# Row factors of the feed-forward parts: one product with a 128x128 block of ones, the Newton steps on all partitions

## The chip, the cores and the metric

One core of one Trainium2 chip runs the kernel. The metric is the device time of one execution in microseconds (us). Three executions of the kernel before took 2188.64, 2190.5 and 2190.98 us; the median is 2190.5 us.

## What is computed

A decoder of two layers over 512 tokens of width 1024, in float32. Each layer is a feed-forward part, a token mixer and a second feed-forward part. Every part begins with an RMS norm: each token (a row of x) is divided by the root of the mean of its squares.

```python
def rms_norm(x, w):
    y = xf * lax.rsqrt(jnp.mean(xf * xf, axis=-1, keepdims=True) + NORM_EPS)
    return y * w

def swiglu_ffn(h, wg, wu, wd):
    return (jax.nn.silu(h @ wg) * (h @ wu)) @ wd

for l in range(DEPTH):
    x = x + 0.5 * swiglu_ffn(rms_norm(x, ffn1_norm[l]), ...)
    x = x + mixed(rms_norm(x, mix_norm[l])) @ w_out[l]
    x = x + 0.5 * swiglu_ffn(rms_norm(x, ffn2_norm[l]), ...)
return rms_norm(x, final_norm)
```

The feed-forward width is 2816. The reciprocal root of a row is a number for each token, and is called its row factor here.

## The kernel before

x stands transposed: eight tiles `x0` to `x7` of 128 features (partitions) by 512 tokens. Matrix products are made in three passes on rounded halves: `xh`, `xl` of x times the norm's weight, and `hi`, `lo` of the weights, so that each 128x128 block of weights costs three products (`mm3`, L217). The row factor is left out of `xh` and `xl`. It is applied to the products: `gated` multiplies `pg` (the gate product in PSUM) by `rstd` on VectorE (`g<-pg,rstd`), takes the silu on ScalarE, multiplies by `rstd` again on GpSimd, and multiplies `pu` (the up product) by the result on VectorE (`u<-pu,g`). `rstd` is therefore a tile of 128x512 with each token's factor in all 128 partitions.

How `rstd` comes about: `square` sums the squares of the eight x tiles into `acc` (128x512). `stats_tok` makes four products with `acc` as the stationary operand and a 128x64 block of 1/1024 (`ones_d`) as the moving one, which gives the mean squares with tokens on partitions (`ps_ms`). It then takes the reciprocal root on VectorE, by a shift and a subtraction on the bits and three Newton steps, on tiles of 128x4 (`ms`, `rs_t`, `rstd_tok`; 12 instructions). `stats_rows` brings the factors back to the layout of the products: four products of `rstd_tok`, broadcast over 128 columns, with the identity (`ps_rb`, L423), and a copy by ScalarE (`rstd<-ps_rb`). Both functions serve the four feed-forward parts and the two mixers; a mixer needs `rstd_tok` for its own products too.

A feed-forward part (`ffn`) goes through the 22 blocks of 128 hidden features in three groups of 8, 8 and 6. For each block `f` TensorE makes `pg` and `pu`, 24 products each, and after a group the eight `pd` (down product), which VectorE adds to x. Some queues matter:

- The products of a group lie in PSUM in a ring of three buffers (`pa`); only in the first group, while `rstd` is not yet there, a few go to a second ring (`pb`). In the first group `hold` is 1 (2 in the very first part): the block 0 products `pg` and `pu` and the block 1 `pg` take the three buffers of `pa`, the block 1 `pu` goes to `pb`, and the block 2 `pg` takes the buffer of the block 0 `pg` again. It can begin only when `g<-pg,rstd` of block 0 has read that buffer.
- Weights come by DMA into `raw`, two blocks at a time; ScalarE rounds a block to `hi` and VectorE (seldom GpSimd) makes `lo<-raw,hi` (`split`). Both have rings of four buffers, so the `hi` of one block waits until TensorE is done with the block four earlier in the order pg0, pu0, pg1, pu1, pg2, ...
- Each engine works through its instructions in one order, fixed when the program is built by the framework's scheduler from priorities and a timeline of its own. `stats_tok` runs under a high priority.

Of the kernel before, what the change touches and what calls it, by code (L numbers as in the profile page):

```python
# [10 lines left out]
F32 = mybir.dt.float32  # L11
# [4 lines left out]
ALU = mybir.AluOpType  # L16
# [3 lines left out]
P = 128  # L20
D = 1024
KD = D // P
T = 512
# [4 lines left out]
EPS = 1e-6  # L28
# [137 lines left out]
class Kern:  # L166
# [9 lines left out]
    def pool(self, name, bufs, **k):  # L176
        return self.tc.tile_pool(name=name, bufs=bufs, reuse_waits="tile", **k)
# [218 lines left out]
    def rsqrt(self, out, v, shape):  # L396

        nc = self.nc
        t = self.tiny.tile(shape, F32, tag="rs_t", name="rs_t")
        nc.vector.tensor_scalar(t.bitcast(I32), v.bitcast(I32), 1, None, ALU.logical_shift_right)  # L400
        nc.vector.tensor_scalar(out.bitcast(I32), t.bitcast(I32), -1.0, 1597463007.0, ALU.mult, ALU.add)
        f = lambda a: a.rearrange("p a b -> p (a b)")
        for _ in range(3):
            nc.vector.tensor_tensor(t, out, out, ALU.mult)
            nc.vector.scalar_tensor_tensor(f(t), f(t), -0.5, f(v), ALU.mult, ALU.mult)
            nc.vector.scalar_tensor_tensor(f(out), f(t), 1.5, f(out), ALU.add, ALU.mult)

    def stats_tok(self):
        nc = self.nc
        with self.tc.high_priority(offset=4000):  # L410
            ps = self.pb.tile([P, NT, 64], F32, tag="b", name="ps_ms")
            for t in range(NT):
                nc.tensor.matmul(ps[:, t, :], self.acc[:, t * P:(t + 1) * P], self.ones_d, start=True, stop=True)
            v = self.tiny.tile([P, NT, 1], F32, tag="ms", name="ms")
            nc.vector.tensor_scalar(v, ps[:, :, 0:1], EPS, None, ALU.add)
            self.rstd_tok = self.tiny.tile([P, NT, 1], F32, tag="rstd_tok", name="rstd_tok")
            self.rsqrt(self.rstd_tok, v, [P, NT, 1])

    def stats_rows(self):
        nc = self.nc  # L420
# [26 lines left out]
    def ffn(self, wg, wu, wd, layer, norm, meanwhile=None, begun=None):  # L447
        nc = self.nc
        xs = list(self.xs)
        for gi, (f0, nf) in enumerate(GROUPS):  # L450
            act, queue = [], deque()
            gu, uu = self.gate_up(wg, wu, gi) if gi or not begun else begun

            hold = 0 if gi else 2 if begun else 1
            for f in range(nf):
                where = lambda i: (self.pb, "b") if 3 <= 2 * f + i <= 2 * hold + 1 else (self.pa, "a")
                pool, tag = where(0)
                pg = pool.tile([P, T], F32, tag=tag, name="pg")
                self.mm3(pg, next(gu), xs, KD)
                if hold and f == hold:  # L460
                    self.stats_rows()
                    while queue:
                        queue.popleft()()
                pool, tag = where(1)
                pu = pool.tile([P, T], F32, tag=tag, name="pu")
                self.mm3(pu, next(uu), xs, KD)
                if hold and f == 0:
                    self.stats_tok()
                queue.append(lambda pg=pg, pu=pu: act.append(self.gated(pg, pu)))
                if f >= hold:  # L470
                    queue.popleft()()
            if gi == 0 and meanwhile:
                with self.tc.issue_after(self.last_load.ins):
                    meanwhile()
            last = gi == len(GROUPS) - 1
            if last and layer == DEPTH:
                return self.end(lambda: self.dense_units(wd[f0 * P:(f0 + nf) * P, :], nf, at=NARROW), act, nf)
            for d, dw in enumerate(self.dense_units(wd[f0 * P:(f0 + nf) * P, :], nf)):
                pd = self.pb.tile([P, T], F32, tag="b", name="pd")
                self.mm3(pd, dw, act, nf)  # L480
                nc.vector.scalar_tensor_tensor(self.x[d], pd, 0.5, self.x[d], ALU.mult, ALU.add)
                if last:
                    self.prepare(d, self.sv[layer][norm])
# [939 lines left out]
    def run(self):  # L1423
        nc, tc, io = self.nc, self.tc, self.io
        with ExitStack() as ctx:
            pool = lambda name, bufs, **k: ctx.enter_context(self.pool(name=name, bufs=bufs, **k))
            dram = ctx.enter_context(tc.tile_pool(name="dram", bufs=1, space=bass.MemoryType.DRAM))
            self.xd = [[dram.tile([P, T], F32, name=f"xd{l}_{d}") for d in range(KD)] for l in range(DEPTH)]
            self.const = pool("const", 1)
            self.pad = pool("pad", 1)  # L1430
            self.pad.tile([P, PAD], F32, name="pad")
            self.xsp = pool("xsp", 1)
            self.wraw = pool("wraw", 2)
            self.whi = pool("whi", W_BUFS)
            self.wlo = pool("wlo", W_BUFS)
            self.tmp = pool("tmp", 1)
            self.m = pool("m", M_BUFS)
            self.mb = pool("mb", 1)
            self.tiny = pool("tiny", 2)
            self.conv = pool("conv", 2)  # L1440
            self.pa = pool("pa", 3, space=PSUM)
            self.pb = pool("pb", 5, space=PSUM)
            self.xs = [None] * KD
            self.new_x()
            self.cst = self.const.tile([P, CST.shape[1]], F32, name="cst")
            self.msk = self.const.tile([P, MSK.shape[1]], U8, name="msk")
            self.ones_d = self.const.tile([P, 64], F32, name="ones_d")
            nc.gpsimd.memset(self.ones_d, 1.0 / D)
            nc.sync.dma_start(self.c("ident"), io["cst"][:, 0:P])
            self.first_vectors()  # L1450
            xt = {}
            begun = self.gate_up(io["ffn1_w_gate"][0], io["ffn1_w_up"][0], 0, 2, (1 if FIRST else 0, 0))
            first = []
            for g in range(2):
                for t in range(NT):
                    xt[t, g] = self.t2("xt")
                    nc.sync.dma_start(xt[t, g], io["x"][0, t * P:(t + 1) * P, g * T:(g + 1) * T])
                if FIRST:
                    if g == 0:
                        w = io["ffn1_w_gate"][0][:, 0:P].rearrange("(k p) f -> p k f", p=P)  # L1460
                        raw = self.wraw.tile([P, KD, P], F32, tag="raw", name="raw")
                        hi, lo = (self.unit(p, tag, [P, KD, P]) for p, tag in ((self.whi, "hi"), (self.wlo, "lo")))
                    for k in range(4 * g, 4 * g + 4, FIRST):
                        ks = slice(k, k + FIRST)
                        nc.sync.dma_start(raw[:, ks, :], w[:, ks, :])
                        nc.scalar.copy(hi[:, ks, :], raw[:, ks, :])
                        nc.vector.tensor_tensor(lo[:, ks, :], raw[:, ks, :], hi[:, ks, :].bitcast(F32), ALU.subtract)
                    if g == 1:
                        first = [(hi, lo), next(begun[1])]
                else:  # L1470
                    first.append(next(begun[g]))
            begun = [chain([u], b) for u, b in zip(first, begun)]
            for d in range(KD):
                ps = self.pb.tile([P, T], F32, tag="b", name="ps_x")
                for t in range(NT):
                    nc.tensor.transpose(ps[:, t * P:(t + 1) * P], xt[t, d // 4][:, d % 4 * P:(d % 4 + 1) * P], self.c("ident"))
                self.split_x(d, ps, self.sv[0]["n1"])
                (nc.scalar.copy if d in XACT else nc.vector.tensor_copy)(self.x[d], ps)
            for d in range(KD):
                self.square(d)  # L1480
            for l in range(DEPTH):
                self.ffn(io["ffn1_w_gate"][l], io["ffn1_w_up"][l], io["ffn1_w_down"][l], l, "nm",
                         *((self.rest, begun) if l == 0 else ()))
                self.spill_x(l)
                self.mix(l)
                self.ffn(io["ffn2_w_gate"][l], io["ffn2_w_up"][l], io["ffn2_w_down"][l], l + 1, "n1")
# [38 lines left out]
```

## Time and profile before

| | |
|---|---|
| times of three executions | 2188.64, 2190.5, 2190.98 us |
| profiled execution: its time | 2192.0 us |
| profiled execution: its span (first to last instruction) | 2190.2 us |
| TensorE's mean granted clock in it | 0.992 of full speed |

The page of the profile gives, for the slowest core, the busy time of each engine (PE is TensorE's products, PEld its weight loads, DVE is VectorE, ACT is ScalarE, POOL is GpSimd), the chain of work that ended last, followed back from the last instruction, and the costliest groups of instructions with the idle time ahead of them and what ended it. Other views list the instructions in order of time, the waits of an engine, and the busy times in chosen stretches. Times are us from the start of the span. All instructions that go through the engine wrappers bear the line L149 (or L146 for tabled activations) of a helper, so they are told apart by their tiles.

By the names in the trace the first feed-forward part runs from the start to about 376 us, layer 0's mixer to about 735, then come the second feed-forward part of layer 0 (to about 1099), the first of layer 1 (to about 1457), layer 1's mixer (to about 1816), and the last feed-forward part with the final norm.

### The profile page before, as it was taken

The numbers are of one execution on the slowest core, as the hardware profiler recorded it, in microseconds if no ns is written. First come the engines' busy times: TensorE is split into PE (matmuls) and PEld (weight loads), VectorE is DVE, ScalarE is ACT, GpSimd is POOL, SyncE is SP. The second block draws the span as 40 slices with busy tenths as digits, with TensorE's granted clock in tenths as the row PEclk, the third lists the DMA queues.
The fourth block names the chain that finished last, engine by engine and source line by source line (L and its number), as shares of the span: only waits on it lengthen the run. The fifth ranks groups of instructions, "written<-read, shape, count | busy, mean of one in ns | idle before, by whom it ended". The sixth has DMA issues, their size and how long they took to land.

```text
span 2190.2 us, 31776 instructions
## 1 busy us (share of the span) xinstructions
PE 2154.9 (98%) x13079; PEld 1829.6 (84%) x13079; DVE 1147.9 (52%) x1980; ACT 842.4 (38%) x1319; POOL 500.4 (23%) x466
## 2 busy tenths in 40 slices
PE   8999999998999999999999999999899999999998
PEld 7888888887988788888888888888889888888888
DVE  5544345468497743433543343364866876434335
ACT  5322224555555422222432222254654544222225
POOL 2201013454333210101211010133633412101011
PEclk9999999999999999999999999999999999999999
DMA  4323234221123323232232322242121232323223
GB/s 155 126 78 116 77 106 140 73 78 40 59 60 106 97 97 96 78 115 80 94 116 96 97 97 96 82 148 79 59 59 40 73 103 88 104 94 99 96 87 126
DMA packets 197757, 203.08 MB, mean 93 GB/s; under 512 B 7626, under 2 KB 189292, under 8 KB 197612
## 3 DMA queue, kind: packets, MB, share of 16 engines
q1 hardware_dynamic: 197612, 201.05, 29.0%
q8 instruction: 103, 1.69, 0.3%
q14 instruction: 42, 0.34, 0.0%
HBM read 194.74 MB, written 6.29 MB: 92 GB/s over the span
## 4 chain that ended last, share of the span: by engine, by line
PE 86%; DVE 9%; ACT 2%; issue 1%; POOL 0%; DMA 0%; SPq 0%; DVEq 0%; ACTq 0%; POOLq 0%
PE pd L217 22%; PE pu L217 22%; PE pg L217 22%; PE ps_fm L260 7%; PE ps_tm L260 5%; PE ps_out L260 2%; DVE aw L149 1%; PE ps_scan L265 1%; DVE lo L149 1%; PE ps_ss L265 1%; DVE blk_p L149 1%; DVE x L149 1%; PE ps_ao L265 1%; DVE flo L149 1%; PE ps_al L265 0%
## 5 line engine op out<-in xcount | busy, mean ns | idle before, releaser
L149 ACT CAST hi<-raw 128x1024 fp32r<-128x1024 f32 (+2 forms) x369 | 379.2, 1028 | 1094.2 <-PE pg L217 323.0
L149 DVE TENSOR_TENSOR lo<-raw,hi 128x1024 fp32r<-128x1024 f32 (+2 forms) x325 | 390.2, 1201 | 80.9 <-ACT hi L149 68.5
L149 POOL TENSOR_TENSOR g<-g,rstd 128x512 f32<-128x512 f32 x88 | 150.2, 1706 | 1130.2 <-ACT g L146 1130.2
L217 PE MATMUL pd<-ah,hi 128*128 128x512 f32 (+1 forms) x752 | 282.0, 375 | 0.0
L217 PE MATMUL pd<-ah,lo 128*128 128x512 f32 (+1 forms) x752 | 281.6, 375 | 0.0
L217 PE MATMUL pd<-al,hi 128*128 128x512 f32 (+1 forms) x752 | 281.6, 375 | 0.0
L217 PE MATMUL pg<-xl,hi 128*128 128x512 f32 x704 | 275.0, 391 | 1.0 <-DVE xl L149 1.0
L217 PE MATMUL pu<-xh,hi 128*128 128x512 f32 x704 | 274.4, 390 | 0.6 <-ACT hi L149 0.6
L217 PE MATMUL pg<-xh,hi 128*128 128x512 f32 x704 | 274.5, 390 | 0.1
L217 PE MATMUL pg<-xh,lo 128*128 128x512 f32 x704 | 274.2, 389 | 0.0
L217 PE MATMUL pu<-xh,lo 128*128 128x512 f32 x704 | 274.1, 389 | 0.0
L217 PE MATMUL pu<-xl,hi 128*128 128x512 f32 x704 | 273.9, 389 | 0.0
L149 DVE TENSOR_TENSOR u<-pu,g 128x512 f32<-128x512 f32 x88 | 60.9, 692 | 280.7 <-PE pu L217 265.2
L149 DVE SCALAR_TENSOR_TENSOR x<-pd,x 128x512 f32<-128x512 f32 (+1 forms) x104 | 67.4, 649 | 229.3 <-PE pd L217 229.0
L149 DVE TENSOR_TENSOR g<-pg,rstd 128x512 f32<-128x512 f32 x88 | 60.8, 691 | 206.8 <-PE pg L217 206.7
L217 PEld LDWEIGHTS pd<-al,hi 128*128 128x128 f32 x752 | 141.4, 188 | 25.7
L217 PEld LDWEIGHTS pd<-ah,lo 128*128 128x128 f32 x752 | 141.3, 188 | 25.4
L217 PEld LDWEIGHTS pd<-ah,hi 128*128 128x128 f32 x752 | 141.1, 188 | 25.5
L217 PEld LDWEIGHTS pg<-xl,hi 128*128 128x128 f32 x704 | 132.3, 188 | 29.3 <-DVE xl L149 2.1
L217 PEld LDWEIGHTS pg<-xh,hi 128*128 128x128 f32 x704 | 132.5, 188 | 27.8 <-ACT xh L149 0.4
L217 PEld LDWEIGHTS pu<-xh,hi 128*128 128x128 f32 x704 | 132.1, 188 | 28.2 <-ACT hi L149 1.0
L217 PEld LDWEIGHTS pu<-xh,lo 128*128 128x128 f32 x704 | 132.3, 188 | 27.5
(331 smaller groups left out, 3778.5 us busy)
## 6 DMA issues: line engine op xcount, KB each, us to landing
raw<-in_ffn_w_gate_dram SPq DMA_DIRECT2D x43, 1024.0 KB, 5.1
raw<-in_ffn_w_up_dram SPq DMA_DIRECT2D x43, 1024.0 KB, 5.1
raw<-in_ffn_w_down_dram SPq DMA_DIRECT2D x32, 1024.0 KB, 4.7
raw<-in_w_in_dram SPq DMA_DIRECT2D x20, 1024.0 KB, 5.2
raw<-in_w_in_dram SPq DMA_DIRECT2D x32, 512.0 KB, 3.6
raw<-in_ffn_w_down_dram SPq DMA_DIRECT2D x20, 768.0 KB, 4.4
xd<-x SPq DMA_DIRECT2D x16, 256.0 KB, 2.5
raw<-in_w_out_dram SPq DMA_DIRECT2D x16, 256.0 KB, 2.6
```

The lines of the kernel that those rows point to most:

```text
L149: return f(*args, **kw)
L217: self.nc.tensor.matmul(ps, a[:, k, :], b, start=n == 0, stop=n == 3 * nk - 1)
L260: self.nc.tensor.matmul(ps, a, b, start=start, stop=stop)
L265: self.nc.tensor.matmul(ps, a, b, start=start, stop=stop)
```

## The change

In the four feed-forward parts `stats_tok` and `stats_rows` are replaced by `stats_all`. One product has a 128x128 block of 1/1024 (`ones_p`) as the stationary operand and `acc` as the moving one; its result `ps_rb` has the mean square of each token in all partitions. The reciprocal root is then taken on VectorE on tiles of 128x512 (`ms_all`, `rs_all`, `rstd`), with the same 12 instructions, and `rstd` needs no copy. `ones_d` becomes the first 64 columns of `ones_p`. The mixers and the final norm are left as they are.

```diff
     def rsqrt(self, out, v, shape):
-        t = self.tiny.tile(shape, F32, tag="rs_t", name="rs_t")
+        f = lambda a: a.rearrange("p a b -> p (a b)")
+        self.newton(f(out), f(v), f(self.tiny.tile(shape, F32, tag="rs_t", name="rs_t")))
+
+    def newton(self, out, v, t):
         nc.vector.tensor_scalar(t.bitcast(I32), v.bitcast(I32), 1, None, ALU.logical_shift_right)
         nc.vector.tensor_scalar(out.bitcast(I32), t.bitcast(I32), -1.0, 1597463007.0, ALU.mult, ALU.add)
         for _ in range(3):
             nc.vector.tensor_tensor(t, out, out, ALU.mult)
-            nc.vector.scalar_tensor_tensor(f(t), f(t), -0.5, f(v), ALU.mult, ALU.mult)
-            nc.vector.scalar_tensor_tensor(f(out), f(t), 1.5, f(out), ALU.add, ALU.mult)
+            nc.vector.scalar_tensor_tensor(t, t, -0.5, v, ALU.mult, ALU.mult)
+            nc.vector.scalar_tensor_tensor(out, t, 1.5, out, ALU.add, ALU.mult)
...
+    def stats_all(self):
+        nc = self.nc
+        with self.tc.high_priority(offset=4000):
+            ps = self.pb.tile([P, T], F32, tag="b", name="ps_rb")
+            nc.tensor.matmul(ps, self.ones_p, self.acc, start=True, stop=True)
+            self.rstd = self.tmp.tile([P, T], F32, tag="rstd", name="rstd", bufs=1)
+            v, t = self.t2("ms_all"), self.t2("rs_all")
+            nc.vector.tensor_scalar(v, ps, EPS, None, ALU.add)
+            self.newton(self.rstd, v, t)
...
                 if hold and f == hold:
-                    self.stats_rows()
                     while queue:
                         queue.popleft()()
...
                 if hold and f == 0:
-                    self.stats_tok()
+                    self.stats_all()
...
-            self.ones_d = self.const.tile([P, 64], F32, name="ones_d")
-            nc.gpsimd.memset(self.ones_d, 1.0 / D)
+            self.ones_p = self.const.tile([P, P], F32, name="ones_p")
+            self.ones_d = self.ones_p[:, 0:64]
+            nc.gpsimd.memset(self.ones_p, 1.0 / D)
```

Since the scheduler sets the order on each engine, the rows below show what it makes of the change. The numbers behind the names are the program's own and differ between the two kernels.

TensorE in the second feed-forward part of layer 0, before: `pg_6870` and `pu_6901` are block 0, `pg_6952` and `pu_6998` block 1, `pg_7037` is the block 2 gate product.

```order
L217 MATMUL pu_6901<-xl6_6852,hi_6904 128x512
L413 MATMUL ps_ms_6932<-ones_d_123,acc_6759 128x64 x4
L217 MATMUL pu_6901<-xh6_6851,lo_6905 128x512
...
L217 MATMUL pg_6952<-xh7_6866,lo_6954 128x512
L423 MATMUL ps_rb_6981<-cst_121,rstd_tok_6939 128x128 x4
L217 MATMUL pu_6998<-xh0_6761,hi_6999 128x512
...
L217 MATMUL pg_7037<-xh0_6761,hi_7040 128x512
```

The same place after the change: `pg_6860` and `pu_6891` are block 0, `pg_6939` and `pu_6978` block 1, `pg_7017` is block 2.

```order
L217 MATMUL pu_6891<-xl6_6842,hi_6894 128x512
L427 MATMUL ps_rb_6922<-acc_6749,ones_p_123 128x512
L217 MATMUL pu_6891<-xh6_6841,lo_6895 128x512
...
L217 MATMUL pg_6939<-xh7_6856,lo_6941 128x512
L217 MATMUL pu_6978<-xh0_6751,hi_6979 128x512
...
L217 MATMUL pg_7017<-xh0_6751,hi_7020 128x512
```

One product of 128x512 stands where four of 128x64 stood, the four of 128x128 ahead of the block 1 `pu` are gone, and the rest keeps its order; `pg_7017` stands right behind the last product of `pu_6978`.

VectorE at the same place before, from the last Newton step on 128x4 on; `lo_7111` belongs to the block 3 `pg` and `lo_7140` to the block 3 `pu`.

```order
L149 SCALAR_TENSOR_TENSOR rstd_tok_6939<-rs_t_6940,rstd_tok_6939 128x4
L149 TENSOR_TENSOR lo_7111<-raw_7038,hi_7110 128x1024
L149 TENSOR_TENSOR g_6988<-pg_6870,rstd_6986 128x512
L149 TENSOR_TENSOR u_6992<-pu_6901,g_6988 128x512
L149 TENSOR_TENSOR al_6995<-u_6992,ah_6994 128x512
L149 TENSOR_TENSOR g_7027<-pg_6952,rstd_6986 128x512
L149 TENSOR_TENSOR lo_7140<-raw_7069,hi_7139 128x1024
```

VectorE there after the change, from the middle of the second Newton step on; `lo_7091` is the block 3 `pg`'s and `lo_7120` the block 3 `pu`'s.

```order
L149 TENSOR_TENSOR rs_all_6926<-rstd_6924 128x512
L149 TENSOR_TENSOR lo_7091<-raw_7018,hi_7090 128x1024
L149 SCALAR_TENSOR_TENSOR rs_all_6926<-rs_all_6926,ms_all_6925 128x512
L149 SCALAR_TENSOR_TENSOR rstd_6924<-rs_all_6926,rstd_6924 128x512
L149 TENSOR_TENSOR rs_all_6926<-rstd_6924 128x512
L149 SCALAR_TENSOR_TENSOR rs_all_6926<-rs_all_6926,ms_all_6925 128x512
L149 SCALAR_TENSOR_TENSOR rstd_6924<-rs_all_6926,rstd_6924 128x512
L149 TENSOR_TENSOR lo_7120<-raw_7049,hi_7119 128x1024
L149 TENSOR_TENSOR g_6968<-pg_6860,rstd_6924 128x512
L149 TENSOR_TENSOR u_6972<-pu_6891,g_6968 128x512
```

The `lo` of the block 3 `pu` stood behind the `g` of block 0 and the `g` of block 1, and stands now ahead of both. The last feed-forward part (layer 1) has the same order as this one.

VectorE in the first feed-forward part of layer 1, before:

```order
L149 TENSOR_TENSOR lo_9429<-raw_9356,hi_9428 128x1024
L149 TENSOR_TENSOR g_9306<-pg_9188,rstd_9304 128x512
L149 TENSOR_TENSOR u_9310<-pu_9219,g_9306 128x512
L149 TENSOR_TENSOR al_9313<-u_9310,ah_9312 128x512
L149 TENSOR_TENSOR g_9345<-pg_9270,rstd_9304 128x512
L149 TENSOR_TENSOR lo_9458<-raw_9387,hi_9457 128x1024
```

and after, where `lo_9399` is the block 3 `pg`'s and `lo_9428` the block 3 `pu`'s:

```order
L149 SCALAR_TENSOR_TENSOR rs_all_9234<-rs_all_9234,ms_all_9233 128x512
L149 TENSOR_TENSOR lo_9399<-raw_9326,hi_9398 128x1024
L149 SCALAR_TENSOR_TENSOR rstd_9232<-rs_all_9234,rstd_9232 128x512
L149 TENSOR_TENSOR g_9276<-pg_9168,rstd_9232 128x512
L149 TENSOR_TENSOR u_9280<-pu_9199,g_9276 128x512
L149 TENSOR_TENSOR lo_9428<-raw_9357,hi_9427 128x1024
```

Here the `lo` of the block 3 `pu` stays behind the `g` of block 0.

No line of the diff touches the mixers, but their instructions come in another order too, on TensorE, VectorE and ScalarE. Before, the two layers' mixers stand in two different orders on TensorE; after the change they stand in one, which is neither of the two.

More of the change, by code (lines that the diff above doesn't have):

```diff
@@ L398, in rsqrt @@
         nc = self.nc
-        t = self.tiny.tile(shape, F32, tag="rs_t", name="rs_t")
+        f = lambda a: a.rearrange("p a b -> p (a b)")
+        self.newton(f(out), f(v), f(self.tiny.tile(shape, F32, tag="rs_t", name="rs_t")))
+    def newton(self, out, v, t):
+        nc = self.nc
         nc.vector.tensor_scalar(t.bitcast(I32), v.bitcast(I32), 1, None, ALU.logical_shift_right)
         nc.vector.tensor_scalar(out.bitcast(I32), t.bitcast(I32), -1.0, 1597463007.0, ALU.mult, ALU.add)
-        f = lambda a: a.rearrange("p a b -> p (a b)")
         for _ in range(3):
             nc.vector.tensor_tensor(t, out, out, ALU.mult)
-            nc.vector.scalar_tensor_tensor(f(t), f(t), -0.5, f(v), ALU.mult, ALU.mult)
-            nc.vector.scalar_tensor_tensor(f(out), f(t), 1.5, f(out), ALU.add, ALU.mult)
+            nc.vector.scalar_tensor_tensor(t, t, -0.5, v, ALU.mult, ALU.mult)
+            nc.vector.scalar_tensor_tensor(out, t, 1.5, out, ALU.add, ALU.mult)
     def stats_tok(self):
@@ L417, in stats_tok @@
             self.rsqrt(self.rstd_tok, v, [P, NT, 1])
+    def stats_all(self):
+        nc = self.nc
+        with self.tc.high_priority(offset=4000):
[5 more added lines that the diff above has]
+            self.newton(self.rstd, v, t)
     def stats_rows(self):
```

## The prediction

> **What bounds the kernel now.** I read the page's busy times and its chain first, then the busy times by stage.
>
> ```profile
> span 2190.2 us, 31776 instructions
> PE 2154.9 (98%) x13079; PEld 1829.6 (84%) x13079; DVE 1147.9 (52%) x1980; ACT 842.4 (38%) x1319; POOL 500.4 (23%) x466
> PE 86%; DVE 9%; ACT 2%; issue 1%; POOL 0%; DMA 0%; SPq 0%; DVEq 0%; ACTq 0%; POOLq 0%
> 376.00:735.00 359.00, 348.23 (x3227) 307.47 (x3227) 251.52 (x577) 192.97 (x367) 144.58 (x167) 0.98 0.23 70
> 735.00:1099.00 364.00, 363.52 (x1612) 301.02 (x1611) 162.48 (x189) 108.10 (x135) 51.66 (x31) 1.00 0.31 99
> 1099.00:1457.00 358.00, 358.00 (x1590) 296.78 (x1589) 150.28 (x175) 102.57 (x127) 49.55 (x29) 1.00 0.32 102
> 1457.00:1816.00 359.00, 347.86 (x3231) 308.64 (x3230) 250.98 (x576) 194.38 (x367) 143.90 (x164) 0.98 0.23 70
> ```
>
> The stage rows give length, then busy PE, PEld, DVE, ACT, POOL, then the granted clock. Where the change acts (rows 735 and 1099) PE is busy for 363.52 of 364 us and all of 358 us: PE bounds these parts. So a product removed there is worth its PE time in full, and any new wait of PE costs in full. VectorE has half of its time free, which matters only where PE waits for it.
>
> **PE's part of the change.** The chain of work in the second feed-forward part of layer 0, in order of time:
>
> ```profile
> 745.88 0.84 PE ps_ms L413 x8
> 746.71 0.99 PE pu L217 x4
> 752.48 0.89 PE ps_rb L423 x8
> 753.37 5.48 PE pu L217 x24
> 758.85 5.44 PE pg L217 x24
> ```
>
> A normal product takes 5.44 / 24 = 0.2267 us. `ps_ms` costs 0.84 plus 0.99 - 4 x 0.2267 = 0.08 of slower products behind it, 0.92; `ps_rb` costs 0.89 + 0.04 = 0.93. Both run as 8 PE instructions for 4 products. A feed-forward part loses 1.85.
>
> The new product of 128x512 is in no row as a plain float32 one. It streams as many columns as the four `ps_rb` products together, in 2 instructions instead of 8. If columns set `ps_rb`'s time, it costs the same 0.93; if weight loads do (`ps_ms` with half the columns costs the same 0.92, which allows that), it could go down to two normal passes, 2 x 0.2267 = 0.45. Above, twice `ps_rb`, 1.86. I take 0.93: the nearest row has the same columns and type. The sum for PE alone is 4 x (1.85 - 0.93) = **-3.7 us** (-5.6 to 0 by the bounds).
> The Trainium skill, "FP8 and Floating Point Precision", section "TensorE Precision Notes", says that true FP32 takes four passes through the array; as an estimate, 4 x 0.2267 = 0.91 for this product and -3.8 for the sum, while the two-pass bound would give -5.6. No run here shows it.
>
> **VectorE's part.** The same 12 instructions, on 512 columns instead of 4.
>
> ```profile
> L149 DVE TENSOR_SCALAR flo<-af 128x512 f32<-128x512 f32 x8 | 3.7, 487 | 0.1
> L149 DVE SCALAR_TENSOR_TENSOR bk<-braw,sv_b,bk 128x512 f32<-128x512 f32 x16 | 12.0, 750 | 9.2 <-POOL bk L149 9.1
> L149 DVE TENSOR_TENSOR g<-pg,rstd 128x512 f32<-128x512 f32 x88 | 60.8, 691 | 206.8 <-PE pg L217 206.7
> 11.79 0.68 DVE L149 COPY x<-ps_x 128x512 f32<-128x512 f32 x1
> 747.68 0.15 DVE L149 TENSOR_SCALAR ms<-ps_ms 128x4 f32<-128x4 f32 x1
> 748.08 0.17 DVE L149 TENSOR_SCALAR rstd_tok<-rs_t 128x4 int32<-128x4 int32 x1
> 748.28 0.16 DVE L149 TENSOR_TENSOR rs_t<-rstd_tok 128x4 f32<-128x4 f32 x1
> 753.37 1.23 DVE L149 TENSOR_TENSOR lo<-raw,hi 128x1024 fp32r<-128x1024 f32 x1 [2.12 <-PE ps_rb L423]
> 754.52 0.68 DVE L149 TENSOR_TENSOR g<-pg,rstd 128x512 f32<-128x512 f32 x1
> ```
>
> Per instruction: `ms_all` reads PSUM, 0.68 as the copy does; the two bit steps have one SBUF source, 0.49 (the integer form is in no row: 0.49 to 0.69); per Newton step one product of two tensors, 0.69, and two of the three-operand kind, 0.75 each. Each needs the one before; the small ones start 0.20 apart and take 0.17, so 0.04 goes between them. That is 0.68 + 0.98 + 3 x 2.19 + 11 x 0.04 = **8.7 us**, against 12 x 0.2 = 2.4. A `lo` among them adds its 754.52 - 753.37 = 1.15. On an engine half free that costs nothing unless `g` of block 0 comes late: PE's block 2 `pg` wants the PSUM buffer that this `g` reads.
>
> **The second feed-forward parts.** Here the order on VectorE puts the `lo` of the block 3 `pu` ahead of that `g`. ScalarE's `hi` for it:
>
> ```profile
> 752.09 0.39 PE L217 MATMUL pg<-xh,lo 128*128 128x512 f32 x1
> 752.32 1.05 PE L423 MATMUL ps_rb<-cst,rstd_tok 128*128 128x128 f32 x8
> 752.29 1.05 ACT L149 CAST hi<-raw 128x1024 fp32r<-128x1024 f32 x1 [3.74 <-PE pg L217]
> 758.66 1.06 ACT L149 CAST hi<-raw 128x1024 fp32r<-128x1024 f32 x1
> 759.86 1.22 DVE L149 TENSOR_TENSOR lo<-raw,hi 128x1024 fp32r<-128x1024 f32 x1
> ```
>
> The `hi` of the block 3 `pg` starts at 752.29, 0.20 after the last product of the block 1 `pg` has started: it waits for the buffer that this product's block used, and its `lo` follows 1.08 later (753.37). By the same ring the `hi` of the block 3 `pu` waits for the end of the block 1 `pu`. Before, that `lo` (759.86) stood behind `g` (754.52) and nobody waited. Now I follow the new order:
> - PE: `ps_rb` of the change stands where `ps_ms` stood and costs as much, so the block 1 `pu` begins at 752.32, its last product at 757.53, and the block 2 `pg` could begin at 752.32 + 5.44 = 757.76.
> - VectorE: `ms_all` from 747.68, a bit step to 748.89, a `lo`, a bit step to 750.57, four Newton instructions to 753.61, the block 3 `pg`'s `lo` (ready at 753.35), five instructions from 754.75 to 758.60.
> - The next `lo` needs the block 3 `pu`'s `hi`: 757.53 + 0.20 = 757.73, + 1.08 = 758.81. Then `g` at 758.81 + 1.15 = 759.96, done at 760.64.
>
> PE starts again at about 760.70 instead of 757.76: a wait of **2.9 us**. Without that `lo`, `g` would end at 759.33 and PE still wait 1.6 us, since the long chain alone is late. Behind the wait nothing hides it, PE being busy to the end of the part. After a wait the first product is slower:
>
> ```profile
> 737.18 0.50 PE L217 MATMUL pg<-xl,hi 128*128 128x512 f32 x1 [0.48 <-DVE xl L149]
> ```
>
> 0.50 instead of 0.39, so 0.1 more. The last part (layer 1) has the same order and the same distances, so both together cost 2 x 3.05 = **+6.1 us**.
>
> **The first feed-forward parts** have cover:
>
> ```profile
> 1104.26 0.16 DVE L149 TENSOR_SCALAR ms<-ps_ms 128x4 f32<-128x4 f32 x1 [4.74 <-PE ps_ms L413]
> 1113.25 1.05 ACT L149 CAST hi<-raw 128x1024 fp32r<-128x1024 f32 x1 [4.44 <-PE pg L217]
> 1114.28 5.48 PE pu L217 x24
> 35.43 1.22 DVE L149 TENSOR_TENSOR lo<-raw,hi 128x1024 fp32r<-128x1024 f32 x1
> 43.23 5.48 PE pu L217 x24
> 44.38 0.69 DVE L149 TENSOR_TENSOR g<-pg,rstd 128x512 f32<-128x512 f32 x1
> ```
>
> In layer 1 the chain starts at 1104.26 and, with two `lo` of 1.15 among its first eleven instructions, reaches 1114.34, when the block 3 `pg`'s `lo` is ready too (1113.25 + 1.08); with this `lo` and the last step `g` ends at 1116.97. The block 1 `pu` now starts about 1 us earlier, at 1113.23, and the block 2 `pg` wants the buffer at 1118.67: 1.7 us in hand. In layer 0 `hold` is 2. `g` of block 0 comes behind a chain that ends at about 45.5 (bit step behind the `lo` of 35.43, one more `lo` in it), done at 46.2, and the block 3 `pg` would start at 43.23 - 0.93 + 5.44 = 47.7: 1.5 us in hand. The copy of `rstd` on ScalarE goes, off PE's path. No cost in either part, unless the chain is over a sixth longer than I make it.
>
> **The mixers** are reordered as a side effect. The two layers' mixers of before had two different orders, and PE idle in them is 359.00 - 348.23 = 10.8 and 359.00 - 347.86 = 11.1 us: unlike orders, like result. I take 0, with 2 us to either side for both together.
>
> **The sum.** -3.7 + 6.1 = +2.4 us on the profiled execution's 2192.0 (span 2190.2 and 1.8 around it); that run is 1.5 above the median of 2190.5, so I put it on the median: **2192.9 us**, +0.11%. A measurement tells apart about 0.2% (4.4 us): below 2186.1 is faster, above 2194.9 slower.
>
> **Rivals.**
> 1. No wait arises: VectorE's chain is shorter than my rows, or `g` gets through in time. Then only PE's saving is left, 2190.5 - 3.7 = 2186.8. For it speaks that the block 1 `pu` gives 5.44 us of cover; against it that the `lo` ahead of `g` starts after that cover's end, however short the chain is. Chance 0.13. With the cheap product (-5.6) it would be 2184.9.
> 2. The wait lowers PE's clock, and the kernel is slower. What waits do to it here:
>
> ```profile
> 502.83 1.31 PE L265 MATMUL ps_al<-aw 128*32 128x16 f32 x128 [3.15 <-DVE a L149]
> 502.50:504.50 2.00, 1.67 (x130) 1.58 (x131) 2.00 (x9) 1.13 (x4) 0.00 (x0) 0.97 0.32 111
> 1582.71 1.78 PE L265 MATMUL ps_al<-aw 128*32 128x16 f32 x128 [3.51 <-DVE a L149]
> 1582.50:1584.50 2.00, 1.79 (x129) 1.75 (x129) 2.00 (x8) 1.12 (x4) 0.00 (x0) 0.62 0.14 46
> 1585.87 0.63 PE L260 MATMUL ps_fm<-xh,hi 128*128 128x512 f32 x1
> 1586.58 0.40 PE L260 MATMUL ps_fm<-xh,lo 128*128 128x512 f32 x1
> ```
>
> After 3.15 us idle the granted clock is 0.97, after 3.51 us it is 0.62, and products take 0.63 instead of 0.39 until about 1586.3. That is 3.6 us at near half speed, a loss of 1.8. My waits are 2.9, under both; the point is between 3.15 and 3.51. If both waits pass it: 2 x 1.8 more, 2190.5 + 6.0 = 2196.5. Chance 0.15.
> The Trainium skill, "TensorE: Matmul & The Clock Gate", section "What's actually happening", puts the half clock after an idle window of about 3.4 us; the trace agrees with its 3.15 and 3.51. By that rule 2.9 us keeps the clock.
> 3. The mixers' new order matters more than I think. The longest wait above, 3.51, arising or going in both layers is 7 us either way: 2185.9 to 2199.9. Chance 0.12, both signs alike.
>
> **How the numbers follow.** The forecast's case has 0.60 and spreads about 2.5 us by the mixers and the product's price (0.45 to 1.86). Slower: nearly all of rival 2, half of 3, a sixth of the forecast's case: 0.30. Faster: half of rival 1 and some of 3: 0.11. Same: 0.59. The range 2186.5 to 2198.0 takes in rival 1 and rival 2 and cuts the tails of 3.
>
> **What would show it.** In the second feed-forward parts PE's block 2 `pg` should wait about 2.9 us for VectorE's `g`, with a `lo` directly ahead of that `g` that waited for ScalarE's `hi`; in the first parts no such wait. `ps_rb` as two PE instructions of about 0.93 together; the chain `ms_all` to `rstd` about 8.7 without its `lo`. The granted clock stays 1.0 behind the waits. Wrong would be: no wait of PE (rival 1), a clock near 0.6 behind it (rival 2), or PE idle in the mixers away from 11 us a layer (rival 3).

## The result, and the profile after

The changed kernel takes **2207.4 us** (median of 6 executions, 2203.2 to 2212.4), the kernel before on the same chip 2190.1 (6 executions, 2188.6 to 2191.3). The ratio is 1.0082, interval 1.0072 to 1.0092: slower by 17 us, where 2 were forecast, and above the range. The profiled execution took 2205.6 us, its span is 2203.9: 13.7 longer than that of before. A second set of 6 executions gave 2211.5 us against 2191.2, ratio 1.0091 (1.0073 to 1.0108).

The page's first part, and the stage rows (length, busy PE, PEld, DVE, ACT, POOL, granted clock):

```profile
span 2203.9 us, 31656 instructions
PE 2160.5 (98%) x13023; PEld 1829.9 (83%) x13023; DVE 1168.0 (53%) x1980; ACT 838.5 (38%) x1315; POOL 496.5 (23%) x466
376.00:735.00 359.00, 346.27 (x3211) 306.34 (x3211) 246.50 (x573) 189.92 (x362) 141.40 (x164) 0.97 0.23 69
735.00:1099.00 364.00, 360.65 (x1575) 297.43 (x1575) 164.05 (x184) 105.44 (x132) 51.65 (x31) 0.99 0.30 96
1099.00:1457.00 358.00, 358.00 (x1580) 296.07 (x1579) 157.00 (x178) 103.14 (x128) 45.07 (x28) 1.00 0.31 100
1457.00:1816.00 359.00, 348.08 (x3218) 308.01 (x3217) 246.09 (x570) 188.74 (x359) 142.91 (x163) 0.97 0.25 75
```

PE has 56 instructions fewer and is busy 5.6 us longer. In row 735 its idle time is 3.35 us where it was 0.48, and the clock is 0.99 where it was 1.00. Row 1099 is as full as before. The stage windows of before no longer fit the stages, so from here on I give a stage's length from the start of its first product to that of the next stage. By that measure the two mixers grew by 3.1 and 3.2 us, the stretch of the second feed-forward part of layer 0 and the first of layer 1 by 4.1, and the last feed-forward part by 3.7; the start is 0.5 shorter.

The chain of work around the second feed-forward part of layer 0 (start, length, what), and VectorE's own rows there:

```profile
748.48 0.86 PE ps_rb L427 x2
749.34 0.93 PE pu L217 x4
755.02 5.23 PE pu L217 x23
760.27 1.05 ACT hi L149
761.35 1.23 DVE lo L149
762.58 0.61 DVE g L149
763.32 8.62 PE pg L217 x24
```

```profile
750.27 0.68 DVE L149 TENSOR_SCALAR ms_all<-ps_rb 128x512 f32<-128x512 f32 x1
752.47 0.42 DVE L149 TENSOR_SCALAR rstd<-rs_all 128x512 int32<-128x512 int32 x1
754.38 0.69 DVE L149 SCALAR_TENSOR_TENSOR rstd<-rs_all,rstd 128x512 f32<-128x512 f32 x1
759.96 0.69 DVE L149 SCALAR_TENSOR_TENSOR rstd<-rs_all,rstd 128x512 f32<-128x512 f32 x1
762.49 0.68 DVE L149 TENSOR_TENSOR g<-pg,rstd 128x512 f32<-128x512 f32 x1
```

The order is the one that the prediction followed: the end of the block 1 `pu`, then `hi`, then `lo`, then `g`, then PE's block 2 `pg`. The chain before had PE alone here. What was not forecast is the last row of the chain: 24 products in 8.62 us, where 24 normal ones take 5.44.

PE's own rows, with what it waited for in brackets, show the wait and where the 3.2 us more in that row come from:

```profile
760.07 0.39 PE L217 MATMUL pu<-xh,lo 128*128 128x512 f32 x1
763.32 0.77 PE L217 MATMUL pg<-xh,hi 128*128 128x512 f32 x1 [2.86 <-DVE g L149]
763.89 0.63 PE L217 MATMUL pg<-xl,hi 128*128 128x512 f32 x1
769.01 0.63 PE L217 MATMUL pg<-xl,hi 128*128 128x512 f32 x1
769.71 0.39 PE L217 MATMUL pg<-xh,hi 128*128 128x512 f32 x1
1851.46 0.68 PE L217 MATMUL pg<-xh,hi 128*128 128x512 f32 x1 [2.86 <-DVE g L149]
```

PE waits 2.86 us in both second parts, and the products behind it take 0.63 instead of 0.39 for some 6 us. That is the half clock of rival 2, behind a wait that I had put on the safe side of its point.

### The profile page after: what moved, and what is told of

Same layout as the page of the kernel before. It is cut to its first block, busy times and chain, and to the rows that moved or that the text cites. A ratio compares the mean times of both kernels' runs of the same rounds, so it can differ in the third digit from the quotient of the medians.

```text
span 2203.9 us, 31656 instructions
## 1 busy us (share of the span) xinstructions
PE 2160.5 (98%) x13023; PEld 1829.9 (83%) x13023; DVE 1168.0 (53%) x1980; ACT 838.5 (38%) x1315; POOL 496.5 (23%) x466
## 4 chain that ended last, share of the span: by engine, by line
PE 88%; DVE 9%; ACT 1%; issue 1%; POOL 0%; DMA 0%; SPq 0%; DVEq 0%; ACTq 0%; POOLq 0%
PE pd L217 22%; PE pu L217 22%; PE pg L217 22%; PE ps_fm L260 8%; PE ps_tm L260 5%; PE ps_out L260 2%; DVE aw L149 1%; PE ps_scan L265 1%; DVE lo L149 1%; DVE x L149 1%; DVE flo L149 1%; PE ps_ss L265 1%; PE ps_ao L265 1%; DVE xl L149 1%; PE ps_al L265 0%
## 5 line engine op out<-in xcount | busy, mean ns | idle before, releaser
L217 PEld LDWEIGHTS pg<-xh,lo 128*128 128x128 f32 x704 | 133.4, 190 | 27.9 <-issue 0.2
```

The lines of the kernel that those rows point to most:

```text
L217: self.nc.tensor.matmul(ps, a[:, k, :], b, start=n == 0, stop=n == 3 * nk - 1)
```

## The experiments

The first theory, after this profile: the wait, the half clock behind it, and the order of the mixers each cost. The rivals: the slow products have another cause than the wait, and the mixers' lengths are chance. All diffs are against the changed kernel, if nothing else is said.

**e1: no wait.** In the parts with `hold` 1 the block 2 `pg` also goes into the larger PSUM ring, so it needs not wait for `g`.

```diff
-where = lambda i: (self.pb, "b") if 3 <= 2 * f + i <= 2 * hold + 1 else (self.pa, "a")
+where = lambda i: (self.pb, "b") if 3 <= 2 * f + i <= 2 * hold + (2 if hold == 1 else 1) else (self.pa, "a")
```

> The change with the block 2 gate product of the three later feed-forward parts put into the second PSUM ring, so that it needs no buffer that g of block 0 must free. If the wait of PE and the clock behind it carry most of the loss, both go: no wait for VectorE's g in the profile, no clock below 0.95 there, and the time falls from about 2207 by 2 x 2.9 plus 2 x (1.9 to 3.6), to about 2193 to 2197 with the mixers as slow as they are, less if layer 1's new order of the mixer is a better one. If the loss is VectorE's longer chain as such, wherever it stands, the time stays above 2200, since the chain is as long as before.

Measured: 2195.4 us, ratio 1.0022 (1.0014 to 1.0030). The wait and the slow products are gone. The middle feed-forward stretch takes 720.6 us (before 722.6) and the last 366.2 (before 367.2): PE's saving, 1.0 for each new part, is there in full. Still the kernel is 5 us slower than before, and mixer 0 takes 366.8 us, where it took 358.8.

**e2: a shorter wait.** The block 3 `pu`'s `lo` is held behind the first `g`, as in the kernel before, so that only the long chain is late.

```diff
-        nc.vector.tensor_tensor(g, pg, self.rstd, ALU.mult)
+        self.first_g = nc.vector.tensor_tensor(g, pg, self.rstd, ALU.mult).ins
...
+                    first = self.first_g
...
-                self.mm3(pu, next(uu), xs, KD)
+                with self.tc.issue_after(first) if hold == 1 and f == 3 else nullcontext():
+                    up = next(uu)
+                self.mm3(pu, up, xs, KD)
```

> The change with the lo (and hi) of the block 3 up product issued behind g of block 0, as before the change. The chain of VectorE alone should still make PE wait, 2.86 - 1.88 = about 1.0 us per second feed-forward part instead of 2.9, and a wait that short should leave the clock at full speed: no granted clock under 0.95 behind it. Layer 0's mixer has the order of the change, layer 1's nearly that of before, so about 2190 - 3.8 + 2.0 + 3.1 = 2191 if the orders of the mixers count by themselves, and about 2188 if they don't. If the lo ahead of g is of no weight, the wait stays at 2.9.

Measured: 2194.0 us, ratio 1.0023 (1.0015 to 1.0032). The view of waits (us in total, times, longest):

```profile
PE pg L217 <- DVE g L149: 2.2, 2, 1.1
```

Two waits of 1.1 us and no slow product behind them. So the `lo` ahead of `g` made 1.8 of the 2.9 us, and these waits of 1.1 kept the clock. The whole time is above both figures that were expected, 2191 and 2188; mixer 0 took 364.1 us.

**e3: the last three parts alone**, with the buffer of e1; the first part is as before. PE's list in the mixers is then that of before, but for two of 3226 instructions in layer 1.

```diff
+                    if not ((layer, norm) in ((1, 'n1'), (1, 'nm'), (2, 'n1'))):
+                        self.stats_rows()
...
-                    self.stats_all()
+                    (self.stats_all if (layer, norm) in ((1, 'n1'), (1, 'nm'), (2, 'n1')) else self.stats_tok)()
```

> The new row factors in the last three feed-forward parts only, with the PSUM room of e1_room; the very first part has the old ones. The mixers come out in nearly the orders of before in both layers. No wait for g, mixers as before: 2190.1 - 3 x 0.95 = 2187.3, faster by about 0.13%. If the mixers' extra time does not come from their order but from what runs ahead of them, it stays here, and the time is 2190 or more.

Measured: 2188.3 us, ratio 0.9995 (0.9986 to 1.0004), 1.0 above the figure expected and not told apart from before. The two feed-forward stretches are those of e1, 720.6 and 366.2.

**e4: the first part alone**, where no wait arises. The three others are as before.

```diff
+                    if not ((layer, norm) in ((0, 'nm'),)):
+                        self.stats_rows()
...
-                    self.stats_all()
+                    (self.stats_all if (layer, norm) in ((0, 'nm'),) else self.stats_tok)()
```

> The new row factors in the very first feed-forward part only, which has no wait in either kernel. Layer 0's mixer then has exactly the order of the change, layer 1's that of e1_room. If the order of the mixers costs by itself, layer 0's is longer by about 3 us than before though nothing else has changed, and the time is about 2190.1 - 0.95 + 3.1 = 2192.3 plus what layer 1's order does. If it does not, 2189.1.

Measured: 2198.1 us, ratio 1.0038 (1.0026 to 1.0050). The three later feed-forward parts take what they took before (722.6 and 367.2), PE has less to do and no new wait in any feed-forward part, and the kernel is 8 us slower. Mixer 0 has the order of the changed kernel here. This speaks for the order of the mixers; together they must have added about 9 us, where 3.1 was expected for mixer 0.

**e5: e1, with the mixers in the order of before.** It also adds the four small products and the small chain of before to the first part; nobody reads their result.

```diff
                 if hold and f == 0:
                     self.stats_all()
+                    if layer == 0:
+                        self.stats_tok()
```

> As e1 (all four parts new, with the buffer that takes the wait away), and the first part also forms the four small products and the small Newton chain of before, whose result nobody reads. That only adds work: about 0.9 us on PE (the price of the four products in the first part of before). But the list of PE's instructions in both mixers is then that of before again (in the second, 6 rows differ). Theory that the ORDER of the mixers costs: mixer 0 falls from 366.8 us in e1 to 356 to 359, mixer 1 stays at 358 to 360; sum 2190.2 - 2.8 = 2187.4 us, range 2185.5 to 2190. Rival, that the mixers' lengths are a matter of chance from run to run and not of the order: 2195.4 + 0.9 = 2196.3 us, or anything between 2190 and 2199.

Measured: 2190.9 us, ratio 1.0002 (0.9994 to 1.0010). It does more work than e1 and is 4.5 us quicker, as the order's theory has it, but 3.5 short of the 2187.4 expected, and mixer 0 took 361.4 us in its profile where 356 to 359 were expected.

**e6: the change with its waits, mixer 0 in the order of before.** The same addition, without e1's buffer.

> The change as it is, its two waits too, with the same unread small products and small chain added to the first part. PE's list in mixer 0 is then that of before, in mixer 1 that of e1 and e4. Theory that the order costs: after 2207.4 + 0.9 (products) - 3.1 (mixer 0 back from 361.9 to 358.8) - 2.2 (mixer 1 from 361.5 to about 359.3, as in e1 and e4) = 2203.0 us; the two waits of 2.9 us and the slow products behind them stay. Rival, that the order of the mixers is nothing: 2208.3 us.

Measured: 2200.9 us, ratio 1.0048 (1.0033 to 1.0062); mixer 0 356.1 us. Both waits are there and half clock behind both. The order's theory had 2203.0, its rival 2208.3. Mixer 0 is back in its old order and mixer 1 in that of e1 and e4: together worth 6.5 us, with 0.9 of added work.

**e7: PE kept busy through the wait.** Twelve products into a bank that nobody reads; `up_last` is the last product of the block before's `pu`.

```diff
+                if hold and norm == "n1" and f == 2:
+                    ps = self.pb.tile([P, T], F32, tag="b", name="ps_fill")
+                    with self.tc.issue_after(up_last):
+                        for _ in range(12):
+                            nc.tensor.matmul(ps, xs[0][0][:, 0:P], xs[0][0], start=True, stop=True)
```

> The change as it is, with 12 products 128x128 by 128x512 into a bank that nobody reads, on PE between block 1's pu and block 2's pg of the two second feed-forward parts. 12 x 0.227 = 2.72 us of work in the 2.86 us wait: what is waited for comes no earlier, but PE does not stand idle. Theory that the idle time itself takes the clock down: no product of the block behind at 0.63 us, the block of pg at 5.4 us instead of 8.6 and 7.3; the stretch of the two middle feed-forward parts falls from 726.7 to 723.5 us, the last from 370.9 to 369.0; with unchanged mixers 2207.4 - 5.1 = 2202.3 us. Rival, that the slow products come from elsewhere (the weights, the buffers, DVE beside them): both stretches as in after, 2207.4 us. Mixer 1 gets an order of its own, so the two stretches decide, not the sum.

Measured: 2197.4 us, ratio 1.0034 (1.0021 to 1.0047). PE's rows at the place:

```profile
757.81 2.88 PE L475 MATMUL ps_fill<-xh 128*128 128x512 f32 x12
760.85 0.47 PE L217 MATMUL pg<-xh,hi 128*128 128x512 f32 x1 [0.15 <-DVE g L149]
761.15 0.39 PE L217 MATMUL pg<-xl,hi 128*128 128x512 f32 x1
```

`pg` starts as late as it did after the wait, but its products take 0.39 at once. The stretches take 723.8 and 369.3 us (expected 723.5 and 369.0; 726.7 and 370.9 in the change): useless work in the gap is worth 2.9 and 1.6 us. **The idle time of PE itself takes the clock down**; the rival with another cause falls.

**e8: the last part alone, with its wait.** The three others and PE's list in both mixers are exactly as before.

```diff
+                    if not ((layer, norm) in ((2, 'n1'),)):
+                        self.stats_rows()
...
-                    self.stats_all()
+                    (self.stats_all if (layer, norm) in ((2, 'n1'),) else self.stats_tok)()
```

> The new rows and the one wait in the last feed-forward part only; the three others as before, PE's list in both mixers exactly that of before. Saved product time -1.0, wait +2.9, and then the slow clock behind it +1.9 to 3.2: the last stretch 367.2 + 3.8 to 5.1 = 371 to 372.3 us, and 2194.0 to 2195.3 us in all. Rival, that the wait costs its own length alone (the clock's part of the loss in after came from the mixers' history): 2190.2 + 1.9 = 2192.1 us.

Measured: 2193.9 us, ratio 1.0019 (1.0011 to 1.0028), with 370.95 us in the last stretch, +3.8: product -1.0, wait +2.9, and 1.9 for the one window of half clock behind it. The rival's +1.9 in all lies below the interval (+2.4 to +6.1).

**The grid.** In all these profiles the stretches of half clock begin at times that lie on a grid of 3.413 us, to 0.12 us, from the first mixer to the last part; most are 3.4 or 6.8 us long, three are 10.2. Laid on that grid, the windows of the changed kernel around the first wait read (length, busy PE first, granted clock third from the end; they are set 0.15 us early, hence 0.52 and 0.98):

```profile
755.72:759.13 3.41, 3.41 (x16) 2.83 (x16) 3.21 (x5) 0.17 (x1) 0.00 (x0) 1.00 0.19 31
759.13:762.55 3.42, 1.33 (x6) 0.75 (x5) 2.65 (x5) 1.04 (x1) 0.00 (x0) 1.00 0.78 275
762.55:765.96 3.41, 2.64 (x6) 2.15 (x7) 1.32 (x3) 0.64 (x2) 1.28 (x1) 0.52 0.67 179
765.96:769.37 3.41, 3.41 (x9) 2.64 (x8) 1.29 (x2) 1.24 (x2) 0.73 (x1) 0.50 0.36 129
769.37:772.79 3.42, 3.42 (x16) 2.77 (x15) 2.03 (x3) 1.61 (x3) 0.55 (x1) 0.98 0.00 0
```

PE was busy 1.33 of 3.42 us, and the next window runs at half clock. The wait reaches 0.77 us into that one, which leaves it 2.64 us of slow work, and the window after it is at half clock too. A window at half clock can lose 3.41 / 2 = 1.7 us. Against the stretches of e1, which have no wait (720.6 and 366.2), the stretches with a wait of 2.86 us show 1.6 to 1.9 us beyond the wait where one window fell, and 3.1 to 3.2 where two did.

Over the windows from mixer 0 to the last part in all 14 profiles, those at full clock with PE busy under 40% of the time were all followed by half clock (64 of 64), those with 70 to 95% never (0 of 218); between, both occur. Of the 6916 windows over 95% busy, 44 were followed by half clock, all in the mixers. The busy time does not explain these, but their work sets them apart: each holds 20 or more instructions of `ps_ss`, products with 16 columns. Of the 50 such windows 44 were followed by half clock, of the other 6866 none. The Trainium skill, "TensorE: Matmul & The Clock Gate", section "What's actually happening", says that the clock is decided on a free-running window of 3413 ns; the trace agrees, with its 3.413.

**e9 and e10** test this on second profiles, of the change and of before.

> The change as it is, once more, for a second profile. Theory (a grid): in the profiles so far every stretch of half clock is 3.4 or 6.8 us long and begins on a grid of 3.413 us that runs freely through the execution, and a grid window in which PE was busy half of the time or less is followed by one at half clock, one with 65% or more at full clock not. So the two waits of 2.86 us stay as long as they were, but each may lose 0, 1 or 2 times 1.7 us behind it, by where it falls on the grid: the stretch of the two middle feed-forward parts 723.3, 725.0 or 726.7 us, the last 369.2, 370.9 or 372.6 us, nothing between; mixer 0 without the clock's loss 351.4 to 352.4 us. 2203 to 2210 us. Rival (the clock's loss is fixed by the length of the wait and what follows): the same 726.7 and 370.9 us as in the first profile.

Measured: 2211.5 us in the median of 6, and 2198.9 in the profiled one: neither is in the range expected. Both waits are 2.86 us again, the stretches 726.6 us (two windows of half clock, 3.4 us by the clock's rows) and 370.9 (one, 1.7). These are the lengths of the first profile again, as both the theory and its rival allow, so e9 does not part the two; e6 (725.3 and 372.2) and the third and fourth profile below do. Mixer 0 took 356.1 us, and 349.3 without the clock's loss: under the 351.4 that I expected, so this profile shows no fixed price of the order apart from the clock.

> The kernel before once more, for a second profile of its mixers. Grid theory: the same instructions in the same order, but other stretches of half clock: mixer 0 loses a multiple of 1.7 us between 3 and 7 times (358.8 us with 5 in the first profile), 350.3 us +- 0.7 without them; the feed-forward stretches 722.6 and 367.2 us to 0.1 us. Rival (the order of the instructions alone sets the stretches): 358.8 us again, with half clock at the same places.

Measured: 2191.6 us; feed-forward stretches 722.6 and 367.2; mixer 0 357.6 us with 6.8 lost to the clock, where the first profile had 358.8 with 8.5. One window of half clock is another one. In before's first profile, and in its second:

```profile
514.63:518.04 3.41, 1.71 (x105) 1.24 (x96) 3.41 (x6) 0.10 (x1) 1.47 (x1) 1.00 0.02 5
518.04:521.46 3.42, 3.42 (x9) 2.68 (x10) 3.42 (x6) 1.05 (x1) 0.00 (x0) 0.50 0.52 153
```

```profile
514.05:517.46 3.41, 2.79 (x176) 2.19 (x176) 3.41 (x8) 1.34 (x2) 2.80 (x4) 1.00 0.02 5
517.46:520.88 3.42, 2.44 (x11) 2.02 (x12) 3.42 (x6) 0.99 (x1) 0.00 (x0) 1.00 0.23 53
```

The same idle time fell into one window in the first (1.71 busy) and was shared by two in the second (2.79 and 2.44), and only the first paid.

**e11 and e12** are two more profiles of the change, to see in which stage its long runs are long.

> The change as it is, a third profile, for the mixers. In its two profiles so far mixer 0 took 361.9 and 356.1 us, mixer 1 361.5 and 361.2 (before: 358.8 and 357.6, 358.3 and 358.2), while most of its runs are longer than the profiled ones (2205.6 and 2198.9 against a median of 2211.5 in the second set). Theory (the order of the mixers makes them longer in most executions, by how many grid windows fall to half clock): the two feed-forward stretches 723.3 to 726.7 and 369.2 to 372.6 us as before, and what the whole run lies above 2203 us is in the mixers, in steps of 1.7 us of lost clock. Rival (the long runs come from longer or colder waits in the feed-forward parts): a run above 2207 us has feed-forward stretches above 726.7 or 372.6 us.

> As e11, a fourth profile: the same two readings. Over the four profiles the theory gives mixer 0 above 359 us in at least two of four, mixer 1 above 360 us in all.

Measured: 2209.8 and 2204.7 us. The middle stretches are 725.3 and 725.1 us, the last 370.7 and 372.2, where the first two profiles had 726.7 and 726.6, 370.9 and 370.9. So the same wait of 2.86 us cost one window in some profiles and two in others, and the longer of the two runs does not get its length from these stretches. Mixer 0 took 365.2 and 359.9, mixer 1 363.9 and 363.8. With the first two profiles, mixer 0 was over 359 in three of four and mixer 1 over 360 in all, as the theory had it.

**What the mixers show together.** The table gives lengths in us; "left" is the median over that of before in the same set, less the change of the two feed-forward stretches, plus 0.9 where the first part has the new product without the old ones beside it: what the mixers must have added. It sets stretches of one profile against a median of several runs, and with a wait a stretch varies by up to 1.6 us.

| kernel | median | mixer 0 | mixer 1 | middle stretch | last | left |
|---|---|---|---|---|---|---|
| mixer 0 in before's order | | | | | | |
| before, e10 | 2190.1 | 358.8, 357.6 | 358.3, 358.2 | 722.6, 722.6 | 367.2, 367.2 | 0 |
| e3 | 2188.3 | 356.0 | 359.7 | 720.6 | 366.2 | 1.1 |
| e5 | 2190.9 | 361.4 | 359.9 | 720.6 | 366.2 | 2.9 |
| e6 | 2200.9 | 356.1 | 360.6 | 725.3 | 372.2 | 2.2 |
| e8 | 2193.9 | 357.4 | 360.9 | 722.6 | 371.0 | -0.8 |
| mixer 0 in the new order | | | | | | |
| the change | 2207.4 | 361.9 | 361.5 | 726.7 | 370.9 | 10.4 |
| e9 | 2211.5 | 356.1 | 361.2 | 726.6 | 370.9 | 13.4 |
| e11, e12 | one run each | 365.2, 359.9 | 363.9, 363.8 | 725.3, 725.1 | 370.7, 372.2 | |
| e1 | 2195.4 | 366.8 | 358.7 | 720.6 | 366.2 | 9.1 |
| e2 | 2194.0 | 364.1 | 359.6 | 722.0 | 366.8 | 5.6 |
| e4 | 2198.1 | 362.6 | 359.8 | 722.6 | 367.2 | 8.8 |
| e7 | 2197.4 | 359.9 | 357.5 | 723.8 | 369.3 | 4.1 |

By single profiles the two groups overlap, as windows fall by chance; by the medians they do not: -0.8 to 2.9 against 4.1 to 13.4. Mixer 0 alone takes 357.9 us in the mean of the six profiles with before's order and 362.1 in the eight with the new one. In mixer 0 the place can be named. PE's rows of the changed kernel there, and of before:

```profile
523.71 1.06 PE L265 MATMUL ps_z<-inv 32*32 32x16 f32 x64 [2.06 <-DVE inv L149]
526.13 1.52 PE L265 MATMUL ps_al<-aw 128*32 128x32 f32 x32 [1.35 <-DVE a L149]
```

```profile
517.92 0.73 PE L260 MATMUL ps_fm<-xh,hi 128*128 128x512 f32 x1 [1.70 <-issue]
```

Two waits, 2.06 and 1.35 us, stand 2.4 us apart. The windows on the grid:

```profile
520.27:523.68 3.41, 1.38 (x7) 0.80 (x5) 3.41 (x6) 0.00 (x0) 0.69 (x1) 1.00 0.50 126
523.68:527.10 3.42, 2.03 (x90) 1.96 (x91) 3.35 (x12) 1.67 (x4) 1.05 (x5) 0.51 0.16 56
527.10:530.51 3.41, 3.41 (x42) 2.79 (x39) 0.86 (x4) 3.24 (x11) 1.91 (x3) 0.50 0.02 5
```

The first wait takes the clock down for two windows. This pair, 2.03 to 2.08 and 1.35 to 1.68 us, is in seven of the eight profiles with the new order of mixer 0, each with one to three windows of half clock around it (1.7 to 5.1 us lost). The eighth is e9, whose mixer was the shortest. In the six with before's order the `ps_z` wait is absent or 0.5 us. The place carries most of the cost. From 515.49 to 535.02 us in before and from 515.01 to 536.67 in the changed kernel PE has the same products in either order: 19.5 and 21.7 us. Over all profiles this stretch takes 18.4 to 19.5 us in before's order, 18.9 in e9, and 21.2 to 23.4 in the seven others: 2.8 of the 4.2 us between the two means of mixer 0.

In mixer 1 the four profiles of the changed kernel take 361.2 to 363.9 us, the ten others, in other orders, 357.5 to 360.9: 3.3 us in the means. Of that 1.1 arises 60 to 72 us into the mixer, where the order is the same in all 14; this piece takes 10.4, 12.0 or 13.6 us as none, one or two windows of half clock fall there. The rest is spread over places where the order differs, 1.1 of it 199 to 238 us into the mixer; no single place stood out.

## Why the prediction was wrong

- **PE's saving** (-3.7) was right. The new product cost 0.86 + 0.93 - 4 x 0.2267 = 0.88, against 0.93 taken; the measured saving per part is 1.0 by the stretches of e1. The Trainium skill's four passes for true FP32 ("FP8 and Floating Point Precision", "TensorE Precision Notes") gave 0.91 as an estimate, and the trace agrees with its 0.88.
- **The wait of the second parts** (2.9 us, twice) was right in place, cause and size. All of that stage is 2.6 us later than in the working, since the mixer was longer; with that, `lo` was due at 758.81 + 2.6 = 761.4 and `g` at 762.6; they came at 761.35 and 762.49. The chain from `ms_all` to `rstd` took 10.38 us with two `lo` in it, 8.1 without, against 8.7: the bit steps were 0.42 and not 0.49, the three-operand steps 0.69 and not 0.75. So the wait without the late `lo` is 1.1 (e2) and not 1.6.
- **The first parts** wait for nothing, as said.
- **The clock behind the wait** is the first step that failed: "My waits are 2.9, under both; the point is between 3.15 and 3.51." There is no such point in the length of a wait. The error is in one reading. I looked at the clock in 502.50 to 504.50, behind the wait of 3.15 us, and saw 0.97. On the grid, before's rows are:

```profile
500.98:504.39 3.41, 1.56 (x129) 1.51 (x130) 3.41 (x10) 1.13 (x4) 0.97 (x2) 1.00 0.55 154
504.39:507.80 3.41, 3.41 (x9) 2.65 (x8) 3.41 (x10) 1.16 (x4) 0.00 (x0) 0.50 0.03 5
```

  The clock did fall behind that wait, at 504.39, and my window ended 0.1 us later. So the trace does not agree with an idle window of about 3.4 us, as the prediction says that it does: a wait of 3.15 us was enough. Rival 2 (chance 0.15) was the case to forecast, with its price about right for one window: 1.8 for each wait was taken, 1.6 to 1.9 was measured where one window fell and 3.1 to 3.2 where two did (two and one, two and one, one and one, one and two in the four profiles of the change). By it the forecast would have been 2192.9 + 3.4 to 5.0 = 2196.3 to 2197.9. The sentence that the Trainium skill's rule "keeps the clock" at 2.9 us took its window as a length of idle time; here it is a window on a grid, in which 2.1 us idle (1.33 of 3.42 busy) is enough.
- **"I take 0, with 2 us to either side" for the mixers** is the second step that failed, and the larger one. Two orders with like idle time were no evidence for a third. The new order of mixer 0 brings a wait of 2.06 us close to one of 1.35, and by the medians the mixers add 10 to 13 us in the changed kernel, 4 to 9 where mixer 0 alone has its order. Rival 3 had named the mixers, with up to 7 us and half of a chance of 0.12.

For the four profiles of the change, mean against mean of before's two: start -1.3, mixer 0 +2.6, middle stretch +3.3, mixer 1 +4.4, last +4.0, together +12.9. The waits and the clock behind them, net of PE's saving, are then 6 of it, the mixers 7. In the medians, which lie above the mean of the profiled runs, the mixers' share is larger by the column "left".

Open stays which of the moved rows in mixer 0 makes the `ps_z` wait, which of them make mixer 1 longer in the changed kernel, and why windows between 40 and 70% busy go one way or the other. Taking all parts but the first with the buffer of e1 (e3) removes both costs and its feed-forward stretches show the saving, but its total can't be told from that of before.

## What to carry to other kernels

A wait of PE is to be priced on the clock's grid: here every wait of 2.86 us cost its own length and then 1.6 to 1.9 us or 3.1 to 3.2 more, while 1.1 us cost nothing more. Read the clock for a full window or two behind a wait before calling it kept. A change that a scheduler spreads over untouched stages needs those stages' new orders followed too: here a saving of 3.7 us in four places cost more in the two mixers that the diff does not touch than in the parts that it does.

## What the runs showed of the hardware

- The clock fell at the end of every window of 3.413 us at full clock in which PE was busy under 40% (64 of 64), and rose only at a later grid point. All 11 waits of 2.86 us, in six profiles, were followed by half clock: for one window where PE was busy over 82% of it, for two where the wait reached over the grid point and left it 74 to 82% (four of the 11). The change's fourth profile has both, one at each wait:

```profile
759.76:763.17 3.41, 2.81 (x7) 2.26 (x8) 1.15 (x2) 0.80 (x2) 1.28 (x1) 0.50 0.68 198
763.17:766.59 3.42, 3.42 (x17) 2.79 (x16) 1.29 (x2) 1.08 (x2) 0.91 (x1) 1.00 0.31 110
1848.60:1852.01 3.41, 2.70 (x7) 2.18 (x8) 1.25 (x2) 0.71 (x2) 1.27 (x1) 0.50 0.66 189
1852.01:1855.42 3.41, 3.41 (x10) 2.67 (x8) 1.29 (x2) 1.17 (x2) 0.80 (x1) 0.50 0.34 119
```

- PE can be busy by the profile and lose the clock all the same: a window at full clock with 20 or more instructions of `ps_ss`, the products with 16 columns, was followed by half clock in 44 of 50 cases, a window over 95% busy with fewer in none of 6866. The kernel before has such a row ahead of its first stretch of half clock in mixer 0, which begins at 439.5 us:

```profile
435.77 2.72 PE L265 MATMUL ps_ss<-ones_d,bsq 128*128 128x16 f32 x23
```

- One program in one order scatters: the change's 14 executions lie between 2198.9 and 2215.1 us, those of before in the same sets between 2185.5 and 2193.7. By the clock's rows the shortest and the longest of the change's four profiles, 10.6 us apart, differ by 8.8 us lost to half clock.
- Twelve useless products in PE's gap made the kernel's middle stretch shorter (726.7 to 723.8 us).
